# V matmuls of the high and low gate parts side by side, 32 tokens by row in the second expert layer, five places for V's tiles, and x loaded behind four modulation tiles

## The chip, the core and the metric

The kernel runs on one core of a Trainium2 chip. The metric is the time of one execution on the device in microseconds, lower is better. The inputs and weights lie in HBM as float32; the result must agree with the float32 reference.

## The reference, cut to what matters

A two-layer block (mixing layers that the change hardly touches, each followed by an expert layer) runs before a second block. All the change's edits but one are in the expert layer `peer`, which runs twice for 256 tokens of 1024 values:

```python
q = jnp.einsum('td,dhk->thk', x_t, w_q).reshape(T, PEER_HEADS, 2, PEER_HALF)
s = jnp.einsum('thpk,hpnk->thpn', q, sub_keys).astype(jnp.float32)
sv, si = lax.top_k(s, K)                       # 16 of 128, for each half
...
fv, fpos = lax.top_k(cand, K)                  # 16 experts of 16384 per token and head
eidx = jnp.take_along_axis(cidx, fpos, axis=-1)
gate = jax.nn.softmax(fv, axis=-1)
u = u_emb[eidx]
v = v_emb[eidx]
act = jax.nn.gelu(jnp.einsum('thkd,td->thk', u, x_t).astype(jnp.float32), approximate=False)
return jnp.einsum('thk,thkd->td', (gate * act).astype(x_t.dtype), v)
```

Around it stands `x = x + g2 * peer(rmsnorm(x) * (1 + sc2) + sh2)`, where `sc2`, `sh2`, `g2` and their like come from `silu(c) @ ada_w`, the modulation.

## The kernel before

**Dense and by row.** Each token uses 8 x 16 = 128 of the 16384 experts. The kernel does not gather for most tokens: for ND = 240 of the 256 tokens it multiplies with all experts. In the U stage 128 tiles of U (128 experts each) give the activations of every expert for the 240 tokens (`lin_t("ut")`, matmuls at L370), and a sparse gate, spread out by small matmuls of one-hot vectors (`spread`, L1010, four tokens a group, 60 groups), zeroes all but the chosen ones. In the V stage the gated activations, tile by tile, are multiplied with the 128 tiles of V. The first SP = 16 tokens of each layer go by row: GpSimd gathers rows of U and V by index (`fetch`, L1076, 128 rows of 4 KB a gather, 16 gathers of U and 16 of V), VectorE multiplies and adds them (L1140, L1147), and a small matmul with `folds` (L1152) adds the result to the V sums.

**Float32 by parts.** Every dense product is made of three matmuls in the reduced format fp32r: high times high, low times high, high times low. ScalarE makes the high part of a weight tile (`whi`, L90), VectorE the low part (`wlo`, L97). In the V stage ScalarE and VectorE split the gated activations in the same way (`split_w`: `gh` L1020, `gl` L1021, 128x240 each). For a tile of V and each of 8 output blocks c of 128 columns, `into` and `mm3` issue L307 (`whi`, `gh`), L308 (`whi`, `gl`) and L309 (`wlo`, `gh`), each with 240 columns moving and a weight load of 128 columns of its own. Two blocks c share one PSUM bank; the V stage holds the four banks of pool `psa`, for all 128 tiles, and `turn_over` adds the sums to x at its end (L577).

**The order.** A `Stream` loads weight tiles on SyncE's queue in a fixed order (L65), as far as its pools have places: `raw` has three, modulation tiles (`ada`) go to `spare` places in the V stages. Three `whi` and three `wlo` buffers lie behind it, so `wlo` of tile i+2 can be written when TensorE has left tile i-1. Engines work in program order. In tile i of the V stage VectorE does first what `bg.pump` gives it of the work by row (one operation for each 1300 ns of credit; 450 ns of credit per tile in layer 0, 600 in layer 1), then `gl` of tile i+2, then `wlo` of tile i+2, with modulation steps (L217) between. The gathers have two places in layer 0 and three in layer 1; a gather is issued when VectorE has done the operation that used its place.

**The start.** SyncE issues `cols`, `ident`, `x` (1 MB) and then 16 modulation tiles of 512 KB. VectorE makes `folds`, then waits for the norm of x (square on ScalarE L2011, sum on TensorE L456, root L462, reciprocal L463, spread L469), multiplies x with it (L2014) and only then takes the 16 modulation steps (L217). The first weight product (L307 with `hh`) needs all 16.

## Time and profile before

| what | value |
|---|---|
| time, median of 3 runs (lowest to highest) | 2401.97 us (2401.54 to 2405.57) |
| profiled execution: its own time, its span | 2400.41 us, 2398.7 us |
| busy share of the span: PE, PEld, DVE, ACT, POOL | 97%, 95%, 78%, 57%, 5% |
| start, until the first weight product | 0 to 37 us |
| first layer's U stage with its routing, V stage | about 110 to 572 us, 572 to 918 us |
| second layer's U stage with its routing, V stage | about 1100 to 1558 us, 1558 to 1912 us |

A matmul's record in the trace is longer than the step from one matmul to the next, because matmuls overlap: L307 to L309 show 276 ns each, while one starts every 112 ns or so. So what a matmul costs is read from the distance of starts in a stretch without waits, not from the mean duration. For VectorE, too, the distance of starts is what an operation costs in a row of others.

### The profile page before, as it was taken

To read this page: it belongs to the slowest core of one execution; us is meant where nothing else is said; L and a number is where in the kernel's file an instruction comes from. 1 tells how busy PE (TensorE), PEld (TensorE's weight loads), DVE (VectorE), ACT (ScalarE), POOL (GpSimd) and SP (SyncE) were. 2 spreads that over 40 slices of the span, in tenths; PEclk is the share of its full clock that TensorE was granted. 3 is DMA by queue.
4 is the path that set the end of the run, shared out by engine and by line. 5 is a ranking of instruction groups with operands and counts; after the bars stand their busy time and mean duration, and the time that the engine had idled before them with its cause. 6 is when DMAs were issued, how large, how long until landed. Compare 5 with 4: busy or idle time off the path is not lost. (4 is left out here: it accounts for less than half of the span.)

```text
span 2398.7 us, 49306 instructions
## 1 busy us (share of the span) xinstructions
PE 2334.3 (97%) x19476; PEld 2282.8 (95%) x19476; DVE 1877.6 (78%) x3608; ACT 1364.8 (57%) x2598; POOL 130.6 (5%) x151
## 2 busy tenths in 40 slices
PE   4999999999999999999999999999999998999998
PEld 4899999999999999889999999999999987999998
DVE  7979888998888878777889789887766677366854
ACT  4565557875554557666565678754455563345543
POOL 0000100000112100000010000012300001000000
PEclk8999999999999999999999999999999999899999
DMA  9666664447999976446566544588876553054664
GB/s 382 241 190 185 203 187 146 141 141 249 326 332 324 324 267 205 149 150 198 179 196 188 173 140 140 175 283 292 296 220 195 185 163 106 4 168 140 182 194 135
DMA packets 134776, 485.26 MB, mean 202 GB/s; under 512 B 16280, under 2 KB 17560, under 8 KB 133648
## 3 DMA queue, kind: packets, MB, share of 16 engines
q1 hardware_dynamic: 122320, 439.53, 56.9%
q0 software_dynamic: 12224, 42.57, 5.2%
q8 instruction: 153, 2.51, 0.4%
q14 instruction: 79, 0.65, 0.1%
HBM read 477.69 MB, written 3.41 MB: 201 GB/s over the span
## 5 line engine op out<-in xcount | busy, mean ns | idle before, releaser
L97 DVE TENSOR_TENSOR wlo<-raw,whi 128x1024 fp32r<-128x1024 f32 x701 | 854.1, 1219 | 259.5 <-ACT whi L90 257.2
L90 ACT ACTIVATE whi<-raw 128x1024 fp32r<-128x1024 f32 x701 | 737.0, 1052 | 251.9 <-DMA raw<-in_v_dram 130.1
L370 PE MATMUL pa<-hh,whi 128*128 128x240 f32 (+2 forms) x2904 | 816.1, 283 | 0.1
L370 PE MATMUL pa<-hl,whi 128*128 128x240 f32 (+2 forms) x2904 | 795.3, 277 | 0.0
L370 PE MATMUL pa<-hh,wlo 128*128 128x240 f32 (+2 forms) x2904 | 793.5, 278 | 0.3 <-DVE wlo L97 0.3
L309 PE MATMUL pa<-gh,wlo 128*128 128x240 f32 x2000 | 551.7, 276 | 4.4 <-DVE wlo L97 3.9
L307 PE MATMUL pa<-gh,whi 128*128 128x240 f32 x2000 | 552.1, 276 | 0.3 <-ACT whi L90 0.3
L370 PEld LDWEIGHTS pa<-hh,whi 128*128 128x128 f32 x2904 | 549.5, 189 | 2.8 <-issue 1.7
L370 PEld LDWEIGHTS pa<-hl,whi 128*128 128x128 f32 x2904 | 549.8, 190 | 1.0 <-DVE hl L581 0.8
L308 PE MATMUL pa<-gl,whi 128*128 128x240 f32 x2000 | 549.7, 275 | 0.0
L370 PEld LDWEIGHTS pa<-hh,wlo 128*128 128x128 f32 x2904 | 544.4, 189 | 0.9 <-DVE wlo L97 0.9
L309 PEld LDWEIGHTS pa<-gh,wlo 128*128 128x128 f32 x2000 | 378.3, 189 | 6.9 <-DVE wlo L97 6.7
L307 PEld LDWEIGHTS pa<-gh,whi 128*128 128x128 f32 x2000 | 379.2, 190 | 0.6 <-ACT whi L90 0.5
L308 PEld LDWEIGHTS pa<-gl,whi 128*128 128x128 f32 x2000 | 378.6, 189 | 0.0
L1003 ACT ACTIVATE hot<-hot,wij 128x128 f32<-128x128 f32 x480 | 153.7, 396 | 40.8 <-DVE hot L995 40.1
L982 ACT ACTIVATE wl<-pa 128x240 f32<-128x240 f32 x144 | 53.3, 370 | 153.0 <-PE pa L370 152.7
L1010 PE MATMUL pb<-hot 128*128 128x128 f32 x960 | 123.2, 275 | 0.0
L1010 PEld LDWEIGHTS pb<-hot 128*128 128x128 f32 x960 | 115.4, 192 | 0.0
L993 DVE TENSOR_TENSOR hot<-iota,wij 128x512 f32<-128x512 f32 x120 | 82.0, 683 | 35.6 <-PE pb L1010 35.6
L1020 ACT ACTIVATE gh<-wu 128x240 fp32r<-128x240 f32 x112 | 45.1, 403 | 112.2 <-PE pa L309 111.1
L1020 ACT ACTIVATE gh<-wl 128x240 fp32r<-128x240 f32 x142 | 56.5, 398 | 70.0 <-PE pa L309 66.1
L995 DVE TENSOR_TENSOR hot<-iota,wij 128x512 f32<-128x512 f32 x120 | 81.9, 682 | 0.0
(579 smaller groups left out, 3205.1 us busy)
## 6 DMA issues: line engine op xcount, KB each, us to landing
raw<-in_ut_dram SPq DMA_DIRECT2D x256, 512.0 KB, 3.7
raw<-in_v_dram SPq DMA_DIRECT2D x256, 512.0 KB, 4.8
sp<-in_ada_dram SPq DMA_DIRECT2D x56, 512.0 KB, 6.5
ada<-in_ada_dram SPq DMA_DIRECT2D x40, 512.0 KB, 10.2
raw<-in_peer_q_dram SPq DMA_DIRECT2D x32, 512.0 KB, 4.3
raw<-in_up_dram SPq DMA_DIRECT2D x32, 512.0 KB, 4.2
raw<-in_down_dram SPq DMA_DIRECT2D x32, 512.0 KB, 4.2
raw<-in_od_in_dram SPq DMA_DIRECT2D x24, 512.0 KB, 4.2
```

What stands on the lines that cost most here:

```text
L90: self.nc.scalar.activation(hi[:, :width], t[:, :width], AF.Copy)
L97: self.nc.vector.tensor_tensor(lo, t, hi, op=OP.subtract)
L307: PE.matmul(ps, lhsT=lh, rhs=rh, start=start, stop=False)
L308: PE.matmul(ps, lhsT=lh, rhs=rl, start=False, stop=False)
L309: PE.matmul(ps, lhsT=ll, rhs=rh, start=False, stop=stop)
L370: PE.matmul(ps, lhsT=part[a], rhs=part[b], start=start and i == 0, stop=stop and i == len(names) - 1)
L982: ACT.activation(t[:, k, gtok:], ps[:, gtok:], AF.Gelu)
L993: V.tensor_tensor(pm, iota[:, None, :].to_broadcast([128, 4, 128]), wij[:, 2, t0:t0 + 4, None].to_broadcast([128, 4, 128]), op=OP.is_equal)
L995: V.tensor_tensor(qm, iota[:, None, :].to_broadcast([128, 4, 128]), wij[:, 1, t0:t0 + 4, None].to_broadcast([128, 4, 128]), op=OP.is_equal)
L1003: ACT.activation(qm[:, j], qm[:, j], AF.Copy, scale=wij[:, 0, t:t + 1])
L1010: PE.matmul(ps[:, j * 128:j * 128 + 128], lhsT=pm[:, j], rhs=qm[:, j], start=True, stop=True)
L1020: ACT.activation(gh, t[:, k], AF.Copy)
```

## The change

1. **Wide V matmuls.** `gh` and `gl` become the two halves of one tile `g` of 2 x ND columns. For a tile i below 108 + c, block c takes one matmul of `whi` with all of `g` and one of `wlo` with its first half. That needs a bank for each c, so the V stage takes the four banks of `psb` besides. At tile 107 + c the two halves of the sum are added to x by VectorE (two operations on ND columns), and from tile 108 + c on the block works with three matmuls as before, starting its sum again in the first half.
2. **SP = 32 in layer 1** (16 stays in layer 0): ND is 224 there, 56 groups of one-hots instead of 60, and 64 gathers and operations by row instead of 32. The gates of 32 tokens lie on 4 x 32 partitions instead of 8 x 16.
3. **Places for V's tiles.** A pool `more`: in layer 1 two tiles from tile 10 on (five places with `raw`), in layer 0 the tile `htok` from tile 72 on, once the gathers of U are used up (four places).
4. **Credits and points.** 400 ns per tile in layer 0 and 760 in layer 1; the work by row is flushed at tile 118 instead of 120; the gain row is made at tile 104 instead of 100; `folds` is made at the start of each V stage instead of at the kernel's.
5. **The start.** Four modulation tiles are issued ahead of x, and eight modulation steps stand ahead of the norm.

```diff
-SP = 16
-ND = S - SP
+SPS = (16, 32)
...
-    vv = w("v", 0)
+    vv = [e[:4] + ("more" if i >= 72 and i % 4 > 2 else "raw",) for i, e in enumerate(w("v", 0))]
...
-    vv = w("v", 1)
+    vv = [e[:4] + ("more" if i >= 10 and i % 5 > 2 else "raw",) for i, e in enumerate(w("v", 1))]
...
-            def split_w(i, gh=None, gl=None):
+            def split_w(i, g=None):
                 t, k = tile_at(i)
...
+                    g = two.tile([128, 2 * ND], FR, name="g", bufs=3)
+                ACT.activation(g[:, :ND], t[:, k], AF.Copy)
+                V.tensor_tensor(g[:, ND:], t[:, k], g[:, :ND], op=OP.subtract)
...
-            order = [(t, k) for t in ("u", "v") for k in range(16)]
+            order = [(t, k) for t in ("u", "v") for k in range(SP)]
...
-            pss = [acc() for _ in range(4)]
...
+            pss = [acc() for _ in range(4)] + [bank() for _ in range(4)]
...
+                pools["more"] = (Slots([two.tile([128, 1024], FT, name=f"more{k}") for k in range(2)]), 2)
...
-                    into(pss, c, w, *parts_of[i], i == 0, i == 127, SP)
+                    g, cs, n = parts_of[i], slice(c * 128, c * 128 + 128), WIDE + c
+                    if i < n:
+                        PE.matmul(pss[c][:, SP:SP + 2 * ND], lhsT=w[0][:, cs], rhs=g, start=i == 0, stop=False)
+                        PE.matmul(pss[c][:, SP:S], lhsT=w[1][:, cs], rhs=g[:, :ND], start=False, stop=i == n - 1)
+                        if i == n - 1:
+                            for a in (S, SP):
+                                o, ps = x[:, c, SP:], pss[c][:, a:a + ND]
+                                V.scalar_tensor_tensor(o, ps, grow[:, c:c + 1], o, op0=OP.mult, op1=OP.add)
+                    else:
+                        mm3(pss[c][:, SP:S], w[0][:, cs], w[1][:, cs], g[:, :ND], g[:, ND:], i == n, i == 127)
...
-                if i == 120:
+                if i == 118:
                     bg.flush()
...
-                    bg.pump(450 if l == 0 else 600)
+                    bg.pump(400 if l == 0 else 760)
...
+    st.load(4)
     nc.sync.dma_start(x, A["x"])
-    V.tensor_reduce(folds, ident.rearrange("p (h t) -> p t h", t=SP), axis=AX.X, op=OP.add)
     st.load()
...
+    for _ in range(8):
+        st.advance()
     rms(rtok, sums(xs))
```

Below, TensorE in the middle of layer 1's V stage, two blocks c of one tile, before (the letters behind `pa_` are the bank's tile, `gh` and `gl` the activations' parts):

```order
L307 MATMUL pa_20221<-gh_21435,whi_21439 128x240
L308 MATMUL pa_20221<-gl_21436,whi_21439 128x240
L309 MATMUL pa_20221<-gh_21435,wlo_21440 128x240
L307 MATMUL pa_20222<-gh_21435,whi_21439 128x240
L308 MATMUL pa_20222<-gl_21436,whi_21439 128x240
```

and after:

```order
L1170 MATMUL pa_19162<-g_19437,whi_19440 128x448
L1171 MATMUL pa_19162<-g_19437,wlo_19441 128x224
L1170 MATMUL pb_19163<-g_19437,whi_19440 128x448
L1171 MATMUL pb_19163<-g_19437,wlo_19441 128x224
L1170 MATMUL pb_19164<-g_19437,whi_19440 128x448
```

Three matmuls per block became two, with two weight loads instead of three, and each block has a bank of its own.

VectorE in layer 1's V stage, before, at the end of the work by row (`sp` with `act` is one such operation, L1147; `gl` and `wlo` prepare tile i+2):

```order
L1021 TENSOR_TENSOR gl_22246<-wl_14000,gh_22245 128x240
L97 TENSOR_TENSOR wlo_22250<-raw_22147,whi_22249 128x1024
L1021 TENSOR_TENSOR gl_22280<-wl_14000,gh_22279 128x240
L97 TENSOR_TENSOR wlo_22284<-raw_22183,whi_22283 128x1024
L1147 SCALAR_TENSOR_TENSOR sp_20228<-sp_20228,act_20343 128x1024
L1021 TENSOR_TENSOR gl_22317<-wl_14000,gh_22316 128x240
L97 TENSOR_TENSOR wlo_22321<-raw_22217,whi_22320 128x1024
```

and after, at tiles 107 to 109, where the first blocks are added to x (L1175):

```order
L1024 TENSOR_TENSOR g_21953<-wu_16337,g_21953 128x224
L96 TENSOR_TENSOR wlo_21957<-more1_19168,whi_21956 128x1024
L1175 SCALAR_TENSOR_TENSOR x_107<-pa_19159,mod_96,x_107 128x224 x2
L1024 TENSOR_TENSOR g_21979<-wu_16337,g_21979 128x224
L96 TENSOR_TENSOR wlo_21983<-raw_21857,whi_21982 128x1024
L1175 SCALAR_TENSOR_TENSOR x_107<-pa_19160,mod_96,x_107 128x224 x2
L1156 SCALAR_TENSOR_TENSOR sp_19146<-sp_19146,act_19246 128x1024
L1024 TENSOR_TENSOR g_22008<-wu_16337,g_22008 128x224
L96 TENSOR_TENSOR wlo_22012<-raw_21883,whi_22011 128x1024
L1175 SCALAR_TENSOR_TENSOR x_107<-pa_19161,mod_96,x_107 128x224 x2
```

The additions to x stand behind `wlo` of tile i+2, and the work by row, which now reaches to these tiles, stands between.

VectorE at the start, before:

```order
L2002 TENSOR_REDUCE folds_92<-ident_86 128x16
L463 RECIPROCAL rtok_100<-rtok_100 128x2
L2014 TENSOR_TENSOR xs_170<-x_108,nrm_99 128x2048
L217 ISA ada_119,mod_97<-ada_119,cact0_154 128x1024
L217 ISA mod_97 128x1
```

and after, from the last of the first eight steps on:

```order
L215 ISA ada_131,mod_96<-ada_131,cact0_152 128x1024
L215 ISA mod_96 128x1
L464 RECIPROCAL rtok_99<-rtok_99 128x2
L2034 TENSOR_TENSOR xs_168<-x_107,nrm_98 128x2048
L215 ISA ada_133,mod_96<-ada_133,cact0_152 128x1024
```

Half of the 16 modulation steps moved ahead of the reciprocal and of the multiplication of x.

## Rows read from the trace of the kernel before

**Rows 1.** The page: busy time, share of the span and instructions of the engines.
```profile
PE 2334.3 (97%) x19476; PEld 2282.8 (95%) x19476; DVE 1877.6 (78%) x3608; ACT 1364.8 (57%) x2598; POOL 130.6 (5%) x151
```
**Rows 2.** Windows (stretch, length, busy PE, PEld, DVE, ACT, POOL; clock, DMA share, GB/s).
```profile
575.00:920.00 345.00, 342.60 (x3032) 340.97 (x3031) 284.76 (x402) 175.23 (x255) 39.11 (x30) 1.00 0.89 310
1360.00:1565.00 205.00, 205.00 (x1819) 205.00 (x1818) 180.31 (x349) 158.49 (x454) 3.32 (x3) 1.00 0.50 153
1565.00:1915.00 350.00, 347.71 (x3077) 346.21 (x3076) 250.84 (x334) 180.31 (x265) 39.42 (x32) 1.00 0.75 246
```
**Rows 3.** Timeline of TensorE (start, duration): 240 columns, V stage, 91 starts.
```profile
599.80 0.27 PE L309 MATMUL pa<-gh,wlo 128*128 128x240 f32 x1
...
609.91 0.28 PE L309 MATMUL pa<-gh,wlo 128*128 128x240 f32 x1
```
**Rows 4.** The same, 512 columns, 58 starts.
```profile
41.73 0.39 PE L307 MATMUL pa<-whi,hh 128*128 128x512 f32 x1
...
54.95 0.39 PE L307 MATMUL pa<-whi,hh 128*128 128x512 f32 x1
```
**Rows 5.** The same, 256 columns, 87 starts.
```profile
2299.80 0.28 PE L307 MATMUL pa<-ah,whi 128*128 128x256 f32 x1
...
2309.98 0.28 PE L309 MATMUL pa<-ah,wlo 128*128 128x256 f32 x1
```
**Rows 6.** The same, 64 columns in float32, nine rows of two; weight loads ahead of 16.
```profile
2097.77 0.39 PE L1869 MATMUL pb<-sa,lt 128*128 128x64 f32 x2
...
2099.78 0.39 PE L1868 MATMUL pb<-vC,mk 128*128 128x64 f32 x2
...
832.03 1.86 PEld L1152 LDWEIGHTS pa<-folds,sp 128*128 128x128 f32 x16
833.81 0.19 PEld L307 LDWEIGHTS pa<-gh,whi 128*128 128x128 f32 x1
```
**Rows 7.** The same, two groups of one-hot matmuls in the U stage.
```profile
1440.09 1.95 PE L1010 MATMUL pb<-hot 128*128 128x128 f32 x16
1441.80 0.36 PE L370 MATMUL pa<-hh,whi 128*128 128x240 f32 x1
```
**Rows 8.** Timeline of the start, all engines (in brackets: idle before, and what ended it).
```profile
7.28 2.55 ACT L2011 ACTIVATE xs<-x 128x256 f32<-128x256 f32 x8
...
13.83 0.17 DVE L463 RECIPROCAL rtok<-rtok 128x2 f32<-128x2 f32 x1 [10.28 <-ACT rtok L462]
...
15.21 2.29 DVE L2014 TENSOR_TENSOR xs<-x,nrm 128x2048 f32<-128x2048 f32 x1 [1.22 <-ACT nrm L471]
17.42 1.22 DVE L217 CUSTOM_DVE_ANT_0 ada<-ada,cact 128x1024 f32<-128x1024 f32 x1
...
28.88 1.06 ACT L90 ACTIVATE whi<-ada 128x1024 fp32r<-128x1024 f32 x1 [13.70 <-DMA ada<-in_ev_in_dram]
...
35.76 0.08 DVE L217 DVE_READ_ACCUMULATOR2_ANT mod<- 128x1 f32 x1
```
**Rows 9.** Windows up to the first layer's U stage (columns as in rows 2).
```profile
10.00:15.00 5.00, 2.87 (x23) 2.48 (x22) 0.17 (x1) 1.75 (x3) 0.00 (x0) 1.00 1.03 415
...
60.00:70.00 10.00, 9.63 (x66) 8.62 (x65) 10.00 (x14) 5.27 (x7) 0.00 (x0) 1.00 1.02 407
```
**Rows 10.** Timeline of VectorE: one operation by row, U's; additions to x.
```profile
1601.56 1.22 DVE L1140 CUSTOM_DVE_ANT_0 rows<-rows,htok 128x1024 f32<-128x1024 f32 x1
...
1602.70 0.40 DVE L1021 TENSOR_TENSOR gl<-wl,gh 128x240 fp32r<-128x240 f32 x1
...
106.02 0.88 DVE L577 SCALAR_TENSOR_TENSOR x<-pa,mod,x 128x256 f32<-128x256 f32 x2
```
**Rows 11.** Timeline of ScalarE and VectorE late in layer 1's V stage.
```profile
1887.91 0.40 ACT L1020 ACTIVATE gh<-wu 128x240 fp32r<-128x240 f32 x1 [1.35 <-PE pa L309]
...
1889.29 1.22 DVE L97 TENSOR_TENSOR wlo<-raw,whi 128x1024 fp32r<-128x1024 f32 x1 [0.54 <-ACT whi L90]
```
**Rows 12.** Time from issue to landing of the gathers, both layers.
```profile
DMA to landing us min/median/max: 5.0/6.8/9.8
```

More of the change, by code (lines that the diff above doesn't have):

```diff
@@ L200, in col @@
         return cols[:, a + i:a + i + n]
-    folds = cst.tile([128, SP], FT, name="folds")
     consts = cst.tile([128, 2], FT, name="consts")
@@ L300, in net @@
     entries += w("up") + w("down")
-    pools = {"raw": (rawp, 3), "ada": (None, 0), "spare": (None, 0)}
+    pools = {"raw": (rawp, 3), "ada": (None, 0), "spare": (None, 0), "more": (None, 0)}
     st = Stream(nc, pools, hip, lop, entries)
@@ L411, in __init__, with block @@
             self.nxt, self.extra = nxt, extra
+        def block(self, c):
+            return block(self.pss, c)
         def mm(self, k, w, c):
@@ L576, in turn_over @@
                 for j in (k, k + 1):
-                    V.scalar_tensor_tensor(x[:, j], block(lk.pss, j), grow[:, j:j + 1], x[:, j], op0=OP.mult, op1=OP.add)
+                    V.scalar_tensor_tensor(x[:, j], lk.block(j), grow[:, j:j + 1], x[:, j], op0=OP.mult, op1=OP.add)
             for j in (k, k + 1):
@@ L937, in peer_route @@
             V.scalar_tensor_tensor(pk[:SP, :, 1], sel[:SP, 0], 128.0, sel[:SP, 1], op0=OP.mult, op1=OP.add)
+            n = SP // 16
             for h in range(8):
-                G.dma_start(picks[h * SP:h * SP + SP], pk[:SP, h])
+                G.dma_start(picks[h // n * SP:h // n * SP + SP, :, h % n * 16:h % n * 16 + 16], pk[:SP, h])
             yield 300
@@ L949, in peer @@
     def peer(l, x, hT, nxt):
+        SP = SPS[l]
+        ND = S - SP
         with ExitStack() as es:
@@ L952, in peer @@
             wl = low.tile([128, I0, ND], FT, name="wl")
-            picks = low.tile([128, 2, 16], FT, name="picks")
-            pick = low.tile([128, 16], I32, name="pick")
+            picks = low.tile([128, 2, SP], FT, name="picks")
+            pick = low.tile([128, SP], I32, name="pick")
             htok = low.tile([128, 1024], FT, name="htok")
@@ L969, in by_token @@
                     ACT.activation(htok[:SP, q * 512:q * 512 + 512], ps[:SP], AF.Copy)
-                for h in range(1, 8):
+                for h in range(1, 128 // SP):
                     G.dma_start(htok[h * SP:h * SP + SP], htok[:SP])
@@ L1053, in route @@
                             yield from peer_top(s_sb, h, b, rs[b], pool)
-                        yield from peer_route(rs[b], wij, pool, b, picks)
+                        yield from peer_route(rs[b], wij, pool, b, picks, SP)
                         if b == 0:
@@ L1096, in peer @@
                     first = again(low, "wij", 3, 256)
-                    split_w(0, first[:, 0, :ND], first[:, 1, :ND])
+                    split_w(0, first.rearrange("p a t -> p (a t)")[:, :2 * ND])
                 old = spread_
@@ L1128, in peer @@
                 rows.places.append(places[2])
+                pools["more"] = (Slots([two.tile([128, 1024], FT, name=f"more{k}") for k in range(2)]), 2)
             def sparse():
-                act = two.tile([128, 16], FT, name="act")
+                act = two.tile([128, SP], FT, name="act")
                 while len(got) < len(rows.places):
@@ L1145, in sparse, with block @@
                         V.tensor_scalar(ysp, r, act[:, 0:1], None, op0=OP.mult)
+                        if l == 0:
+                            pools["more"] = (Slots([htok]), 1)
                     else:
                         V.scalar_tensor_tensor(ysp, r, act[:, k:k + 1], ysp, op0=OP.mult, op1=OP.add)
-                    if n + ahead < 32:
+                    if n + ahead < len(order):
                         got.append(fetch(*order[n + ahead]))
                     yield 1300
-                for c in range(8):
-                    PE.matmul(block(pss, c)[:, :SP], lhsT=ysp[:, c * 128:c * 128 + 128], rhs=folds, start=False, stop=False)
-                yield 0
+            folds = two.tile([128, SP], FT, name="folds")
+            V.tensor_reduce(folds, ident.rearrange("p (g t) -> p t g", t=SP), axis=AX.X, op=OP.add)
             bg.set(sparse())
             class Outs:
-                def __init__(self):
-                    self.pss = pss
                 def mm(self, i, w, c):
-                    into(pss, c, w, *parts_of[i], i == 0, i == 127, SP)
+                    g, cs, n = parts_of[i], slice(c * 128, c * 128 + 128), WIDE + c
[8 more added lines that the diff above has]
+                        mm3(pss[c][:, SP:S], w[0][:, cs], w[1][:, cs], g[:, :ND], g[:, ND:], i == n, i == 127)
+                def block(self, c):
+                    return pss[c][:, :S]
                 def finish(self, c):
@@ L1174, in peer @@
             for i in range(126):
-                if i == 100:
+                if i == 104:
                     grow = ada_done(l, 5)
-                if i == 120:
+                if i == 118:
                     bg.flush()
+                    for c in range(8):
+                        PE.matmul(pss[c][:, :SP], lhsT=ysp[:, c * 128:c * 128 + 128], rhs=folds, start=False, stop=False)
                 if i == 124:
@@ L1192, in peer @@
                 parts_of.pop(i)
-            pools["spare"] = (None, 0)
+            pools["spare"] = pools["more"] = (None, 0)
             sq = wu.rearrange("p i t -> p (i t)")[:, :2048].rearrange("p (k t) -> p k t", k=8)
```

12 lines of the change are left out of this document (4 added, 8 removed).

## The prediction

> **What bounds the kernel now.** First the page's busy times: TensorE 97%, its weight loads 95%, VectorE 78% [rows 1]. Then windows by stage, since an average hides stages: in both V stages, and in the U stage with one-hots, TensorE is busy at full granted clock nearly all the time, while VectorE has 17 to 28% of the V stages free [rows 2]. So a microsecond off TensorE's queue in these stages is a microsecond off the end, as long as nobody else becomes late. The start is another matter: there TensorE waits for VectorE.
>
> Then the real price of a matmul, from distances of starts: 240 columns, 10.11 us over 90 steps, 112.3 ns [rows 3]; 256 columns, 10.18 over 86, 118.4 ns [rows 5]; 512 columns, 13.22 over 57, 231.9 ns [rows 4]. From 256 to 512 that is 0.443 ns a column. But the line doesn't go on below 240: records with 64 columns take 2.01 us over 18 steps, 111.7 ns, and sixteen weight loads for matmuls of only 16 columns take 1.78 us, 111 ns each [rows 6]. What is common to them is a weight load of 128 columns. I read this as a floor: a matmul with its own full weight load costs some 111.5 ns, however few columns move. At 240 columns kernel and floor are level. This decides what each half of the change is worth.
>
> **The change part by part.**
> *Wide matmuls, layer 0.* Sum over c of (108 + c) is 892 blocks with two matmuls, 132 keep three. Before, 3 x 112.3 = 336.9 ns. After, 480 columns by the line between 256 and 512: 118.4 + 224 x 0.443 = 217.6, and 240 columns 112.3; together 329.9. Saved: 7.0 ns x 892 = 6.2 us. Bounds of the unseen 480: twice the 240, 224.6, saves nothing; 256's price plus its columns at the slope between 240 and 256 (6.1 ns / 16 = 0.38), 203.5, saves 18.8 us. I take the line, since both its ends are measured.
>
> *Wide matmuls, layer 1.* 448 columns: 118.4 + 192 x 0.443 = 203.5; 224 columns: the floor, 111.5. Together 315.0, saved 21.9 x 892 = 19.5 us; the 132 triples save 3 x 0.8 each, 0.3 us. Here 32 tokens by row pay: the wide matmul is 32 columns shorter and not on the floor. Bounds: 209.6 for 448 (twice 112.3 less 32 x 0.468, the 240's price per column) with 112.3 leaves 13.4 us; 191.4 by the slope 0.38 leaves 30.3.
>
> *U stage, layer 1.* 128 x 8 x 3 = 3072 matmuls go from 240 to 224 columns. By the floor they save 0.8 ns each, 2.5 us; nothing if the floor is 112.3; 18.7 us if the slope 0.38 went on. I take 2.5, because 64 and 16 columns cost the same [rows 6]. Four groups of one-hots fewer: two groups take 1.71 us [rows 7], so 3.4 us off TensorE, which was busy all 205 us there [rows 2].
>
> The Trainium skill ("TensorE: Matmul & The Clock Gate", LDWEIGHTS) gives a load as its columns divided by 1.2, 106.7 ns for 128. The rows lie at 111 to 112; by the page's figure the 3072 would cost 5.6 ns less each, 17 us in place of 2.5, and the sum below would be lower by that. The measured floor decides, and nothing below uses the page.
>
> *Start.* x now lands behind 2.1 MB of modulation, which at 415 GB/s [rows 9] is 5.1 us. The squares start at 12.4 instead of 7.28 [rows 8]; the reciprocal came 6.55 us after that, now at 18.9. The eight steps ahead of it need four more tiles behind x, again 5.1 us, so the last ends near 17.5 + 1.15 = 18.6: level, they hide in the 10.28 us that VectorE was idle. Then 1.38 to the multiplication, 2.21 for it, and eight steps of (35.76 - 17.42) / 16 = 1.146: 18.9 + 1.4 + 2.2 + 9.2 = 31.7, against 35.76. 4.1 us earlier. The first weight tile is there at 28.88 [rows 8], so it isn't late next. Afterwards VectorE is busy without gaps [rows 9], so what it gains stays; DMA is full at 407 GB/s too, which is the lower bound (nothing gained, if tiles come no earlier). Upper bound: half the steps off, 9 us.
>
> *Additions to x, new.* At tile 107 + c VectorE adds two halves to x, and block c's next matmul, one tile later, waits for them. Two such operations cost 0.88 us in a row at 256 columns [rows 10]. They stand behind `wlo` of tile i+2, which starts 1.38 us after its tile's turn of the buffers and takes 1.14 [rows 11]: done some 2.5 us into the tile, 3.4 with the additions. TensorE is back at block 0 after 8 x 0.33 = 2.64 us in layer 0 and 2.52 in layer 1: it waits about 0.9 us once; for later c its way is 0.3 us longer each and the wait fades. In layer 1 the work by row still runs here (1.14 us an operation [rows 10], one in 1.7 tiles), behind which `g` and `wlo` of the next tile queue. I put 1.5 us for layer 0, 2.5 for layer 1; bounds 0 and 8 x 0.88 = 7 each.
>
> *Work by row, layer 1.* 32 more operations of 1.14 us are 36.5, the additions 7 more. VectorE goes from 251 to about 294 us, over a stage that shrinks to 330: 89%, layer 0 was at 83% without loss [rows 2]. A late gather holds VectorE, and `g` and `wlo` behind it, then TensorE. I put 2.5 us. The bytes grow by 32 gathers of 0.52 MB to some 310 GB/s, what layer 0 carried on three places; five places cover a landing that gets longer. `folds` costs two small reductions, hidden or 0.4 us; the other edits nothing, since the flush at 118 finds the work by row already done (64 x 1300 / 760 = 110 tiles).
>
> *Sum.* 6.2 + 19.5 + 0.3 + 2.5 + 3.4 + 4.1 = 36.0 off; 1.5 + 2.5 + 2.5 + 0.4 = 6.9 on; 29.1 net. From the profiled execution's 2400.4 that is 2371.3; the median of the runs was 1.6 higher, so **2373 us**.
>
> **Rivals.**
> *No floor, columns alone set the price.* For: 240 to 256 still costs 0.38 ns a column. Against: rows 6. The U stage would give 18.7 instead of 2.5, the 224s in V 892 x 5.3 = 4.7 more, the triples 2: 23 lower, 2350. [...]
>
> *Wide matmuls cost what their columns cost at 240.* For: between 256 and 512 the price per column is hardly lower (0.453 against 0.463). Then the doing away with a weight load gives nothing in layer 0 (6.2 lost) and 13.4 - 19.5 in layer 1: 2385. This is the case in which the first edit doesn't do what it seems made for.
>
> *The gathers become the bound, slower.* Layer 1 has three places for 64 gathers. One operation in 1.7 tiles of 2.52 us is one in 4.3 us, so a place must turn round in 12.9: issue and landing, now 6.8 in the median and 9.8 at most [rows 12], the operation, and the queue on VectorE. With 3 us for the last two, it decides from a landing of about 10 us. If the fuller DMA made it 13, a turn would be 16, 5.3 us an operation, and the stage 64 x 1.0 = 64 us longer: 2437. Against: the longest landing seen, under the heavier load of layer 0 included, stays just below the point, and landing in the median has 3 us to spare.
>
> *The start gains nothing* because the DMA queue is the bound: 2377, inside the range.
>
> **How the numbers follow.** Forecast, with small errors of each term: 0.69. Columns alone: 0.10. Wide matmuls at 240's rate: 0.13. Gathers: 0.08, half of it mild (a few us to 35 lost), half beyond. The forecast's own range is 2362 to 2383. To hold 0.8 with a part of both neighbours I take 2354 to 2388. A measurement tells 0.2%, 4.8 us, from no change: faster than 2397 in all of the first three and some mild gather cases, 0.93; same 0.03; slower than 2407 0.04.
>
> **What would show it.** In the V stages, starts 217 ns after a 480-column matmul and 203 after 448, and 111 to 112 after a 224-column one; in layer 1's U stage still 111 to 113 a step. Steps of 105 to 107 there mean columns alone; 224 after 480 means the second rival. At the start, the last of 16 modulation steps near 31.7. At tiles 108 to 112, waits of TensorE's wide-to-narrow change for the additions to x, about 1 us at most. In layer 1's V stage, VectorE waiting for gathers, and TensorE for `wlo` by more than 5 us in all, would show the third rival. If V's gain in layer 1 is there and the total is not, I have mis-seen a wait behind the stages.

## The result, and the profile after

The changed kernel takes **2367.76 us** in the median of four runs (2366.22 to 2369.46), the kernel before 2401.76 beside it (four runs, 2393.81 to 2405.57): a ratio of 0.9868, 95% interval 0.9852 to 0.9883, 34 us less. In the larger groups of runs below, the kernel before has medians of 2398.26 to 2400.23, which would make it 30.5 to 32.5 us less. The forecast was 2373, with a range of 2354 to 2388. The profiled execution shown here took 2369.46 us, its span is 2367.8, 30.9 below the span of before.

The page first: busy time, share of the span and instructions of each engine, against [rows 1].

```profile
PE 2304.9 (97%) x17660; PEld 2210.4 (93%) x17660; DVE 1914.7 (81%) x3673; ACT 1351.0 (57%) x2578; POOL 211.3 (9%) x179
```

TensorE has 1816 matmuls fewer and is busy as large a share as before; VectorE has 37 us more to do in a shorter span. So the kernel is bound as it was. The windows of layer 0's V stage and of layer 1's U stage and V stage (columns as in [rows 2]):

```profile
575.00:905.00 330.00, 324.67 (x2012) 293.94 (x2012) 278.49 (x398) 164.56 (x241) 41.95 (x30) 1.00 0.88 314
1360.00:1550.00 190.00, 190.00 (x1703) 189.98 (x1702) 167.71 (x322) 144.11 (x420) 3.25 (x3) 1.00 0.47 155
1550.00:1880.00 330.00, 327.88 (x2192) 312.67 (x2192) 285.29 (x394) 175.25 (x263) 118.37 (x62) 1.00 0.87 315
```

The third line is the one to look at. VectorE went from 72% to 86% of that stage, the DMA from 246 to 315 GB/s, and TensorE still waits for only 2 us of 330. In the first line TensorE waits for 5.

Where the time went, by landmarks, each the first or last start of a line of matmuls in the two traces:

| stretch | before | after | difference |
|---|---|---|---|
| start to first score matmul (first scores of layer 0) | 126.3 | 125.4 | -0.9 |
| from there to the first one-hot matmul of layer 0 | 242.7 | 243.8 | +1.1 |
| from there to the first attention matmul behind layer 0 (the end of its U stage, its V stage, and 83 us more) | 637.4 | 636.8 | -0.6 |
| last score matmul to last one-hot matmul of layer 1 (U stage) | 387.6 | 379.3 | -8.3 |
| from there to an attention of the second block (V stage of layer 1, and some 255 us more) | 625.9 | 602.6 | -23.3 |
| first to last V matmul of layer 0 alone | 351.5 | 352.0 | +0.5 |
| first to last V matmul of layer 1 alone | 350.8 | 330.8 | -20.0 |

Layer 1 has it all in this pair of traces. Of its last stretch, 20.0 us lie in the V stage itself and 3.0 behind it, where nothing was edited. The prices behind it, from distances of starts as in [rows 3 to 5]. Timeline of TensorE in layer 0, the first rows of 61 and the last one:

```profile
599.77 0.38 PE L1170 MATMUL pb<-g,whi 128*128 128x480 f32 x1
599.99 0.28 PE L1171 MATMUL pb<-g,wlo 128*128 128x240 f32 x1
600.10 0.38 PE L1170 MATMUL pb<-g,whi 128*128 128x480 f32 x1
...
609.75 0.38 PE L1170 MATMUL pa<-g,whi 128*128 128x480 f32 x1
```

Thirty pairs in 9.98 us: 332.7 ns a pair, 220 for the wide matmul and 112 for the other. The forecast was 329.9. The same for layer 1, from the first wide matmul to the eightieth:

```profile
1599.88 0.37 PE L1170 MATMUL pb<-g,whi 128*128 128x448 f32 x1
1600.09 0.27 PE L1171 MATMUL pb<-g,wlo 128*128 128x224 f32 x1
1600.19 0.37 PE L1170 MATMUL pb<-g,whi 128*128 128x448 f32 x1
...
1624.81 0.37 PE L1170 MATMUL pb<-g,whi 128*128 128x448 f32 x1
```

79 pairs in 24.93 us: 315.6 ns, forecast 315.0. The split is another than forecast (212 and 103, against 203.5 and 111.5), the sum is right.

### The profile page after: what moved, and what is told of

Its sections match the earlier page's. It is cut to its first block, busy times and chain, and to the rows that moved or that the text cites. A ratio compares the mean times of both kernels' runs of the same rounds, so it can differ in the third digit from the quotient of the medians.

```text
span 2367.8 us, 46020 instructions
## 1 busy us (share of the span) xinstructions
PE 2304.9 (97%) x17660; PEld 2210.4 (93%) x17660; DVE 1914.7 (81%) x3673; ACT 1351.0 (57%) x2578; POOL 211.3 (9%) x179
## 5 line engine op out<-in xcount | busy, mean ns | idle before, releaser
L368 PE MATMUL pa<-hh,whi 128*128 128x224 f32 (+3 forms) x2904 | 813.5, 282 | 0.2 <-ACT hh L545 0.2
L368 PE MATMUL pa<-hl,whi 128*128 128x224 f32 (+3 forms) x2904 | 794.5, 277 | 0.1
L368 PE MATMUL pa<-hh,wlo 128*128 128x224 f32 (+3 forms) x2904 | 792.1, 278 | 1.5 <-DVE wlo L96 1.5
L1170 PE MATMUL pb<-g,whi 128*128 128x480 f32 (+1 forms) x900 | 304.1, 378 | 0.0
L1170 PE MATMUL pa<-g,whi 128*128 128x480 f32 (+1 forms) x868 | 293.9, 378 | 0.0
L1171 PE MATMUL pb<-g,wlo 128*128 128x240 f32 (+1 forms) x900 | 242.9, 270 | 0.0
L1171 PE MATMUL pa<-g,wlo 128*128 128x240 f32 (+1 forms) x868 | 235.3, 271 | 4.2 <-DVE wlo L96 4.1
L1170 PEld LDWEIGHTS pb<-g,whi 128*128 128x128 f32 x900 | 169.4, 188 | 20.8
L1171 PEld LDWEIGHTS pa<-g,wlo 128*128 128x128 f32 x868 | 165.2, 190 | 7.9 <-DVE wlo L96 7.6
L1171 PEld LDWEIGHTS pb<-g,wlo 128*128 128x128 f32 x900 | 171.1, 190 | 0.0
L1014 PEld LDWEIGHTS pb<-hot 128*128 128x128 f32 x928 | 111.7, 192 | 0.0
```

The lines of the kernel that those rows point to most:

```text
L368: PE.matmul(ps, lhsT=part[a], rhs=part[b], start=start and i == 0, stop=stop and i == len(names) - 1)
L1014: PE.matmul(ps[:, j * 128:j * 128 + 128], lhsT=pm[:, j], rhs=qm[:, j], start=True, stop=True)
L1170: PE.matmul(pss[c][:, SP:SP + 2 * ND], lhsT=w[0][:, cs], rhs=g, start=i == 0, stop=False)
L1171: PE.matmul(pss[c][:, SP:S], lhsT=w[1][:, cs], rhs=g[:, :ND], start=False, stop=i == n - 1)
```

## The experiments

All are the kernel before or the changed kernel with one thing undone, doubled or taken away. The ratios are to the kernel before, timed in the same group of runs.

**1. Which part brings it: 16 tokens by row in layer 1.** The changed kernel with SP = 16 in both layers. The two extra places of layer 1 don't fit into SBUF then, because the tiles of 2 x 240 columns are larger, so layer 1 gets layer 0's form, `htok` as a fourth place from tile 72 on.

```diff
-SPS = (16, 32)
+SPS = (16, 16)
-    vv = [e[:4] + ("more" if i >= 10 and i % 5 > 2 else "raw",) for i, e in enumerate(w("v", 1))]
+    vv = [e[:4] + ("more" if i >= 72 and i % 4 > 2 else "raw",) for i, e in enumerate(w("v", 1))]
-                    bg.pump(400 if l == 0 else 760)
+                    bg.pump(400)
```

> The changed kernel with 16 tokens by row in layer 1 too (credit 400 there; without the shorter gate tiles there is no room for two more places, so V has a fourth place from tile 72 on, as in layer 0). Theory (a matmul costs its columns or, below some 240, its weight load of about 112 ns; wide matmuls save the third load): layer 1 goes the way of layer 0, a block costs 332.7 ns in place of 315.3, so its V stage is about 16 us longer than in the changed kernel (346 for 330), its U stage 9 us longer (113.6 ns a step for 111.7, four groups more): about 2393 us, that is 8 us under before or less. Rival (the gain of layer 1 comes from the wide matmuls and the places as such, not from the tokens): V stage of layer 1 still 335 us or less, about 2375 us.

Measured: 2391.07 us, before 2398.26; ratio 0.9975 (0.9963 to 0.9988). The U stage of layer 1 took 387.6 us, as before, and the V stage with what follows 616.5, 9.4 less than before (the V stage alone 344.5). So about a fifth of the gain, 7 of 34 us, comes with 16 tokens by row; the rest needs the 32. It is not the two places that this kernel lacks: these are all of TensorE's waits in layer 1's V stage, and they are for the additions to x.

```profile
PE pa L305 <- DVE x L1171: 1.3, 2, 1.0
```

**2. No wide matmuls.** The changed kernel with three matmuls a block throughout, all else kept.

```diff
-                    if i < n:
-                        PE.matmul(pss[c][:, SP:SP + 2 * ND], lhsT=w[0][:, cs], rhs=g, start=i == 0, stop=False)
-                        PE.matmul(pss[c][:, SP:S], lhsT=w[1][:, cs], rhs=g[:, :ND], start=False, stop=i == n - 1)
...
-                    else:
-                        mm3(pss[c][:, SP:S], w[0][:, cs], w[1][:, cs], g[:, :ND], g[:, ND:], i == n, i == 127)
+                    mm3(pss[c][:, SP:S], w[0][:, cs], w[1][:, cs], g[:, :ND], g[:, ND:], i == 0, i == 127)
```

> The changed kernel without wide matmuls: three matmuls of 224 or 240 columns per block throughout, nothing added to x ahead of the end; 32 tokens, places, start kept. Theory: a block of layer 1 costs 3 x 111.7 = 335 ns in place of 315.3, 17.6 us more over 892 blocks, less 3 us of waits for the additions; layer 0 is unchanged, since what its wide matmuls save (3.8 us) is spent in waits: about +15 us, 2383. Rival (columns alone set the price): a block of 3 x 224 columns would cost what 448 + 224 cost, and the time stays within 4 us of the changed kernel's 2368.

Measured: 2383.57 us, ratio 0.9939 (0.9919 to 0.9959). In layer 1 the V stage takes 344.8 us against 330.8 with wide matmuls: they are worth 14.0 us there (15.7 with what follows). In this kernel 2958 matmul records fill layer 1's V window without a gap:

```profile
1550.00:1880.00 330.00, 330.00 (x2958) 330.00 (x2956) 273.84 (x360) 165.90 (x247) 77.10 (x62) 1.00 0.87 308
```

**3. Three places for V's tiles.** The changed kernel without `more` in both layers.

```diff
-    vv = [e[:4] + ("more" if i >= 72 and i % 4 > 2 else "raw",) for i, e in enumerate(w("v", 0))]
+    vv = w("v", 0)
-    vv = [e[:4] + ("more" if i >= 10 and i % 5 > 2 else "raw",) for i, e in enumerate(w("v", 1))]
+    vv = w("v", 1)
```

> The changed kernel with V's tiles in three places throughout. Theory (the places are needed, since gathers and tiles together move 315 GB/s in layer 1 and a place must turn round in 3 x 2.52 = 7.6 us): TensorE waits for wlo in layer 1's V stage by 5 to 25 us, ScalarE waits for V's tiles in more than half the tiles; 2373 to 2393 us. Rival (places are cover that nothing needs): within 2 us of 2368, waits of TensorE for wlo under 3 us.

Measured: 2400.28 us, ratio 1.001 (0.9994 to 1.0025). More than expected: without the places **nothing is left of the gain**. The window of layer 1's V stage, and the longest waits of ScalarE and of the weight loads in it (time, number, longest):

```profile
1550.00:1880.00 330.00, 312.76 (x1968) 289.29 (x1966) 267.60 (x370) 163.68 (x243) 105.21 (x63) 0.99 0.84 301
```

```profile
ACT whi L89 <- DMA raw<-in_v_dram: 114.3, 76, 4.2
...
PEld pa L1171 <- DVE wlo L96: 19.0, 24, 1.3
```

In the changed kernel the first of these is 5.5 us, in 5 waits. The chain is landing, `whi`, `wlo`, TensorE: TensorE is the last in it, and it waits 17 us in this window. The V stage of layer 1 takes 355.8 us, 25 more than in the changed kernel. That of layer 0, which has three places throughout here as well, takes 354.0; the mean of five with the fourth place is 348.7.

**4. Is it three, four or five?** The changed kernel with one extra place in layer 1 in place of two.

```diff
-    vv = [e[:4] + ("more" if i >= 10 and i % 5 > 2 else "raw",) for i, e in enumerate(w("v", 1))]
+    vv = [e[:4] + ("more" if i >= 10 and i % 4 > 2 else "raw",) for i, e in enumerate(w("v", 1))]
-    pools["more"] = (Slots([two.tile([128, 1024], FT, name=f"more{k}") for k in range(2)]), 2)
+    pools["more"] = (Slots([two.tile([128, 1024], FT, name=f"more{k}") for k in range(1)]), 1)
```

> The changed kernel with four places for V's tiles in layer 1 (one extra place, every fourth tile from 10 on) in place of five; three gave 2400. Theory: what counts is whether a place can turn round, landing (4.5 us in the median before) plus the wait for ScalarE and the two splits (some 3 us), within the number of places times a tile's 2.52 us: 7.6 for three, too little, 10.1 for four, enough in the median. So most of the 32 us comes back: 2368 to 2376. Rival: the longest landings decide, not the median, and each place gives its share, so about half comes back: 2380 to 2388.

Measured: 2366.05 us (2363.41 to 2370.55), before 2400.23; ratio 0.9864 (0.9838 to 0.989), the same as with five. ScalarE waits 9.7 us for V's tiles in that stage, in 9 waits, and TensorE is busy for 326.98 of 330:

```profile
1545.00:1875.00 330.00, 326.98 (x2184) 311.50 (x2183) 284.91 (x393) 175.80 (x262) 114.29 (x62) 1.00 0.86 314
```

The step lies between three and four; the fifth place buys nothing that can be measured. That fits the theory that a place must turn round within the places times a tile's 2.52 us, though the theory's own sum does not decide it: landing, 4.5 us in the median in layer 1's V stage of before, and about 3 for ScalarE's and VectorE's splits (1.05 and 1.22 us) and their queues make 7.5, level with the 3 x 2.52 = 7.6 that three places give. Experiment 3 shows the turn: 355.8 us for 128 tiles are 2.78 us a tile, so three places turned round in 8.3 us in the mean. Four places give 4 x 2.52 = 10.1.

**5. 32 tokens by row in layer 0 too.**

```diff
-SPS = (16, 32)
+SPS = (32, 32)
-                    bg.pump(400 if l == 0 else 760)
+                    bg.pump(760)
```

> The changed kernel with 32 tokens by row in layer 0 too (credit 760, two places for its 64 gathers, three for V's tiles up to tile 72, 40 modulation steps besides). Rival (TensorE alone bounds both V stages): layer 0's U stage 9 us and its V stage 15 us shorter, 2344 us. Theory (VectorE and the gathers' turn bound that stage: 278 + 38 us of VectorE in a stage of some 330, a gather's place must turn round in 2 x 4.3 = 8.6 us against a landing of 7 plus the operation): the U stage gives 9 us, the V stage gives nothing or gets longer by up to 25 us, with TensorE waiting for wlo by more than 15 us: 2360 to 2385 us.

Measured: 2391.21 us, ratio 0.9971 (0.9958 to 0.9984). Layer 0's V stage, with its two gather places and 48 modulation steps in it, takes 383.3 us, 31.3 more than in the changed kernel; 5.5 of them come back at the end of the U stage, with its four groups of one-hots fewer. In the window TensorE is busy for 296 of 330, and VectorE waits for gathers:

```profile
575.00:905.00 330.00, 295.96 (x1758) 267.93 (x1757) 285.96 (x410) 149.50 (x219) 121.09 (x61) 0.97 0.92 342
```

```profile
DVE sp L1156 <- DMA rows<-in_v_dram,pick: 19.4, 15, 3.8
PE pa L1171 <- DVE wlo L96: 18.4, 26, 1.7
```

This is the forecast's third rival, the gathers as the bound, in the layer that has two places for them. Is it near in layer 1 too?

**6. Two gather places in layer 1.** The changed kernel with one place taken away.

```diff
-                rows.places.append(places[2])
```

> The changed kernel with two places for gathered rows in layer 1's V stage in place of three. An operation of the work by row comes every 4.3 us, so a place must turn round in 8.6 us; landing took 6.8 us in the median and 9.8 at most before, the operation 1.1. Theory of the third rival (a gather that is late holds VectorE, and wlo behind it, then TensorE, nearly one for one): about 8 to 9.5 us a turn, 64 operations, 0 to 30 us slower, about 15: 2383. Other theory: VectorE's 12% of free time and the three g tiles ahead take it up, 2368 to 2371.

Measured: 2402.88 us, before 2399.49; ratio 1.0022 (1.0009 to 1.0035), all of the gain gone again, a little beyond the upper end expected. From layer 1's last one-hot matmul to the second block's attention it takes 638.8 us, 36.2 more than the changed kernel, 32.9 of them in the V stage itself. VectorE's waits in that stage:

```profile
DVE sp L1155 <- DMA rows<-in_v_dram,pick: 29.9, 19, 3.9
DVE rows L1145 <- DMA rows<-in_u_dram,pick: 24.8, 13, 4.0
```

In the changed kernel VectorE has no wait for a gather there. The 64 operations run from 1551.1 to 1857.2 us, 63 steps of 4.86 us: two places turn round in **9.7 us**. With three places, in the changed kernel, they run from 1557.4 to 1830.5, 4.33 us a step, which is the pace that the credits set; a turn could last 13.0. So the rival's mechanism is real, and three places stand 3 us away from it.

**7. The floor, further down.** The changed kernel with 64 tokens by row in layer 1: 192 columns in the U stage, 384 and 192 in V.

```diff
-SPS = (16, 32)
+SPS = (16, 64)
-                    bg.pump(400 if l == 0 else 760)
+                    bg.pump(400 if l == 0 else 1500)
```

> The changed kernel with 64 tokens by row in layer 1 (credit 1500), so that the U stage's matmuls have 192 columns and V's 384 and 192. Theory (a matmul with its own weight load of 128 columns has a floor near 111.6 ns): a step of the U stage stays at 111 to 112 ns at 192 columns. In the V stage 128 operations of 1.14 us bring VectorE from 285 to about 358 us of work, above TensorE's some 290, and three gather places have to turn round 128 times: that stage takes 30 to 75 us longer, the one-hots some 7 us less: 2390 to 2440. Rival (columns alone set the price): a step of the U stage falls to about 98 ns, 3072 of them save 40 us, and the time is 2350 to 2400.

Measured: 2461.14 us, ratio 1.0258 (1.0232 to 1.0284), 21 us beyond the upper end expected. The U stage settles the floor. Timelines of TensorE in the U stage, 137 starts each, first the changed kernel and then this one:

```profile
1171.81 0.27 PE L368 MATMUL pa<-hh,whi 128*128 128x224 f32 x1
...
1186.99 0.27 PE L368 MATMUL pa<-hl,whi 128*128 128x224 f32 x1
```

```profile
1171.75 0.28 PE L368 MATMUL pa<-hl,whi 128*128 128x192 f32 x1
...
1186.94 0.27 PE L368 MATMUL pa<-hh,wlo 128*128 128x192 f32 x1
```

15.18 and 15.19 us over 136 steps, 111.6 and 111.7 ns: 32 columns fewer bring nothing. By columns alone it would have been 98. The Trainium skill ("TensorE: Matmul & The Clock Gate", LDWEIGHTS) puts the load of 128 columns at 106.7 ns; the step measured here is 5 ns longer.

In the V stage of this kernel the same 192 columns stand behind a wide matmul, and there they go below that floor: from the second row to the third it is 90 ns (89 in the median), from the first to the second 200 (198).

```profile
1565.86 0.36 PE L1170 MATMUL pa<-g,whi 128*128 128x384 f32 x1
1566.06 0.25 PE L1171 MATMUL pa<-g,wlo 128*128 128x192 f32 x1
1566.15 0.36 PE L1170 MATMUL pa<-g,whi 128*128 128x384 f32 x1
```

In the V stage as a whole the gathers pace VectorE: the operations run from 1545.0 to 1926.5 us, 127 steps of 3.00 us, a turn of 9.0 us for three places, and TensorE is last in line. It stands idle for 74 of the 420 us, and its granted clock (first of the last three columns) is 0.90 in the mean; how much that adds to the time is not known.

```profile
1540.00:1960.00 420.00, 346.29 (x2117) 327.95 (x2115) 348.49 (x477) 166.00 (x253) 224.68 (x126) 0.90 0.88 323
```

**8. The start alone.** The kernel before with the new order of the start.

```diff
     nc.sync.dma_start(ident, A["ident"])
+    st.load(4)
     nc.sync.dma_start(x, A["x"])
...
         ACT.activation(xs[:, k], x[:, k], AF.Square)
+    for _ in range(8):
+        st.advance()
```

> The kernel before with one part of the change alone: x behind four modulation tiles, and eight modulation steps ahead of the row sums. Theory: the DMA queue is full from 10 to 90 us in both kernels, so VectorE's earlier steps are given back while it waits for tiles. The first weight product then starts near 34.5 us (37.1 before), the first score matmul (line 840) near 125.4 (126.2 before), the first hot matmul (line 1010) at 369.0 within 0.5, and the time is that of before within 1 us (about 2400). Rival (my forecast): the 2.5 us or more stay: first score matmul near 123.5, hot near 366.5, time about 2397.

One execution: 2393.46 us. First weight product at 33.8 us (37.1 before), first score matmul 124.5 (126.3), first one-hot matmul 367.1 (369.0). So 3.2 us at the first product, and nearly half of it lost by the time of the scores; that lies between the theory and the rival. The total was lower than that explains, because the stretch with layer 0's V stage, where nothing was edited, took 633.2 us and not 637.4. So the same kernel was run more often:

> The kernel of the first look at the start alone once more, timed in rounds. That look showed the first weight product 3.2 us earlier, the first score matmul 1.8 us and the first hot matmul 1.9 us earlier, and a further 4 us in layer 0's V stage, where the edit changes nothing. Theory: the edit is worth 1 to 2 us, the rest is scatter between executions: ratio 0.9985 to 1.0. Rival: the 4 us belong to it too: ratio near 0.997.

Measured: 2397.87 us (12 runs), before 2400.23 (16 runs); ratio 0.999 (0.9977 to 1.0003). Its first score matmul starts at 125.4 in that profile. By the landmarks the edit is worth 1 to 2 us. The time alone says less: its interval reaches from 5.5 us gained to 0.7 lost, so it excludes neither nothing nor the 4.1 of the forecast. The rival's ratio of 0.997 lies just outside it, so the 4 us of layer 0 are scatter as far as this shows.

**9. Why half of it is lost.** Two kernels, with the old and with the new start, that load only half of each of the first 40 modulation tiles.

```diff
+            if j < 40:
+                for _ in range(2):
+                    V.tensor_tensor_reduce(t[:, :512], t[:, :512], cact[0][:, :512], scale=1.0, scalar=0.0,
+                                           op0=OP.mult, op1=OP.add, accum_out=mod[:, j:j + 1])
+                return
...
+            return [(("ada", l * 48 + j), A["ada"][l * 48 + j][:, :512], 512, ada_step(l * 48 + j), src) for j in js]
```

> The kernel before, but of the first 40 modulation tiles only the first 512 of 1024 columns are loaded, and each step is taken twice over that half, so that VectorE's columns stay the same while the bytes of this stretch fall by 40 x 0.26 = 10.5 MB, 25 us at 408 GB/s (half of the modulation's input is left out of the sum, so the output isn't the reference's). It is the partner of the next kernel; what counts is the difference of the two. Theory (DMA is the bound of the first 90 us): the first score matmul moves from 126.2 to about 115 or less, until VectorE's steps (1.15 us, 40 of them) are the bound. If DMA isn't the bound, it stays at 124 to 127.

> The same halved modulation tiles, with the changed start (x behind four tiles, eight steps ahead of the row sums); half of the modulation's input is left out of the sum here too. Theory (bytes gave the gain back): with fewer bytes the queue runs ahead, and the changed start keeps 2 to 4 us at the first score matmul against the kernel with the old start. Rival (something behind the start, not the bytes, sets the time): the two agree within 1 us at the first score matmul, as they do with whole tiles.

Measured: 2409.13 us with the old start, 2399.12 with the new one, one execution each. My first expectation missed: the score matmul did not come earlier with half the bytes but later, at 136.0, because two half steps take VectorE 1.35 us from start to start where a whole one takes 1.15, 8 us over 40 tiles, and VectorE became the bound. With half tiles the new start keeps all that it gains: first weight product 41.7 and 34.6 (-7.2), first score matmul 136.0 and 128.9 (-7.1), first one-hot matmul 379.2 and 371.4 (-7.8). The DMA share (last column but one) falls as well. From 10 to 90 us, the changed kernel and the one with half tiles and the new start:

```profile
10.00:90.00 80.00, 56.69 (x299) 49.10 (x300) 71.05 (x123) 37.63 (x63) 0.91 (x1) 0.81 1.01 404
```

```profile
10.00:90.00 80.00, 54.12 (x281) 46.05 (x282) 72.15 (x177) 36.90 (x62) 1.39 (x1) 0.83 0.83 290
```

But the pair does not show that the bytes take the gain. The queue is full with whole tiles, yet between 38 and 90 us neither TensorE nor VectorE nor ScalarE waits for a DMA, in the kernel before, in the changed one or in the two executions of experiment 8. What differs is the clock of TensorE over its first 16 weight products, 512 columns each. In this order the kernel before, the changed kernel, half tiles with the old start, half tiles with the new one (granted clock: first of the last three columns):

```profile
37.06:42.66 5.60, 5.54 (x16) 4.05 (x17) 5.10 (x10) 5.50 (x11) 0.00 (x0) 0.70 1.03 410
34.48:41.40 6.92, 6.86 (x16) 5.02 (x17) 6.07 (x12) 6.50 (x11) 0.00 (x0) 0.54 1.03 410
41.74:47.66 5.92, 5.86 (x16) 4.30 (x17) 5.41 (x10) 5.83 (x11) 1.36 (x1) 0.65 0.84 257
34.58:40.64 6.06, 6.00 (x16) 4.37 (x17) 5.56 (x10) 5.97 (x11) 1.39 (x1) 0.64 0.87 281
```

In each of them TensorE comes out of 13 us of idle time or more at a granted clock of 0.50 (1.2 GHz) and later rises to 1.00 (2.4 GHz), at 40.4, 40.8, 45.9 and 39.0 us. So it runs its products at the low level for 3.4 us before and 6.3 after, and the same 16 products take 1.3 us longer: half of the 2.6 us gained. With half tiles the two stretches happen to be alike, 4.1 and 4.4 us, and the loss is 0.1. In all ten executions with whole tiles and the new start the 16 products take 6.8 to 7.1 us. With whole tiles and the old start there is only the one trace, so how often its low stretch is as short as 3.4 us is not known.

## Why the prediction was right, and where its terms were off

The direction, the mechanism and the total were right: 2373 for 2367.76, and 29.1 us net for the 34 measured (30.5 to 32.5 beside the larger groups of before). That the total came so near is partly luck, since the terms are off with both signs. The two profiles side by side, and the means of all the profiles whose code is that of before or that of after in the stretch (how many, in brackets):

| stretch | forecast, net | two profiles | means |
|---|---|---|---|
| start, to the first scores | -4.1 | -0.9 | -1.1 (1 and 10) |
| V stage, layer 0 | -4.5 | +0.5 | -1.3 (5 and 5) |
| U stage, layer 1 | -5.9 | -8.3 | -8.3 (6 and 6) |
| V stage, layer 1 | -14.6 | -20.0 | -17.3 (5 and 3) |

(The forecast's 0.4 for `folds`, half in each V stage, is counted in.) The V stages go from the first to the last V matmul. Behind each of them the changed kernel gains another 1.5 to 2 us in the means, up to the next attention. The forecast has no term for that, and no run shows where it comes from.

**Wide matmuls, layer 1: right.** Before, the steps that do not follow a wait have a mean of 112.3 ns over the whole stage, as in [rows 3]; after, a block costs 315.6 ns over all 892. That makes 21.3 x 892 = 19.0 us, forecast 19.5. Two of the signs named did not come, 203 ns after 448 columns and 111 to 112 after 224: it was 212 and 103. Only the sum was right. That is more than chance, since it holds at three shapes: 332.3 ns for 329.9 at 480 and 240 columns, 315.6 for 315.0 at 448 and 224, 287 for 286.6 (the same line and floor) at 384 and 192. Why the wide matmul takes up what the narrow one gives is not shown.

**The rest of layer 1's V stage: the term that failed is the wait for the work by row.** I charged 2.5 us for it and 2.5 for the additions. All of TensorE's waits in that stage after, by reason:

```profile
PE pa L305 <- DVE x L1175: 1.8, 3, 1.2
PE pa L1171 <- DVE wlo L96: 0.3, 1, 0.3
```

The first are the additions, in the place and of the kind that was forecast: the longest first, 1.2 us, then fading. With the slower steps right behind each wait they cost 2.5 us, as charged. The work by row cost at most the 0.9 us that is left of the slow steps, and VectorE has no wait for a gather. In the trace of before the waits of that stage, with the slow steps behind them, come to 4.2 us and in that of after to 3.4. So 19.0 + 0.2 for the triples + 4.2 - 3.4 = 20.0, which is the whole of what the stage lost. But 4.2 belongs to one execution. TensorE's busy time in this stage in the trace of before, and in one of experiment 9 with the same code there:

```profile
1558.30:1909.20 350.90, 348.63 (x3091) 347.40 (x3090) 249.28 (x331) 180.59 (x265) 39.35 (x32) 1.00 0.76 249
1570.60:1917.50 346.90, 346.90 (x3091) 346.82 (x3090) 249.54 (x331) 181.14 (x265) 39.34 (x31) 1.00 0.76 252
```

In four other executions with the code of before the waits cost 0.3 to 2.7 us. So it is not shown that the extra places took waits away that were there before; they are cover, as forecast. Experiment 3 shows how far the cover is from nothing: its absence costs 32 us, and I had named the landing that "gets longer" without a price for it.

**U stage, layer 1: right in kind, too small.** Four groups of one-hots were 3.4, measured 3.3. For the 3072 matmuls I took the floor for what they cost after, and it was right (111.6, forecast 111.5). What they cost before was mis-sized, 113.6 and not 112.3, in 135 starts in the trace of before:

```profile
1171.76 0.28 PE L370 MATMUL pa<-hh,whi 128*128 128x240 f32 x1
...
1186.98 0.28 PE L370 MATMUL pa<-hh,wlo 128*128 128x240 f32 x1
```

I had carried a price from the V stage to the U stage, in which the same 240 columns run 1 ns slower. From the last score to the last one-hot matmul 2944 of the matmuls took 337.5 us before and 332.5 after, 5.0 in place of 2.5, and 5.0 + 3.3 is the 8.3 of the landmarks. The floor itself, the choice against the first rival, is settled by experiment 7; the rival's 2350 is refuted.

**Wide matmuls, layer 0: half of it.** 480 columns took 220 ns and not 217.6, and the pair 332.3, so it saves 336.9 - 332.3 = 4.6 ns, 4.1 us in place of 6.2. From that come off the additions, 2.3 us with the slow steps behind them (forecast 1.5). That leaves 1.8, less `folds`. The two profiles show nothing of it, because TensorE waited longer for `wlo` in that of after:

```profile
PE pa L1171 <- DVE wlo L96: 3.8, 7, 0.8
```

In experiment 6, whose layer 0 has the same code, the same wait is 0.6 us. The stage scatters from one execution to the next: 346.4 to 352.0 us in five with wide matmuls, 346.7 to 352.7 in five with the code of before. The difference of the means, 1.3 us, is no surer than that. Layer 0 is the layer with three places, four in its second half, at 314 GB/s; with three throughout (experiment 3) it took 354.0.

The second rival (wide matmuls at 240's price per column) would have made 480 columns cost 224.6, and 220 lies between it and the forecast; in layer 1, where 448 and 224 cost 315.6 together and not the 321.9 of that rival, it is wrong.

**Start: the step that failed.** The forecast said that VectorE is busy without gaps afterwards, "so what it gains stays", and put a full DMA queue as the lower bound. It followed VectorE alone and had no term for TensorE's clock, and the clock took a part of the gain twice. The rows of before that [rows 8] leave out, row sums and first weight product:

```profile
7.83 4.32 PE L456 MATMUL pb<-consts,xs 128*128 128x128 f32 x32 [1.08 <-ACT xs L2011]
...
37.06 0.80 PE L307 MATMUL pa<-whi,hh 128*128 128x512 f32 x1 [22.30 <-ACT hh L498]
```

The same after, with the reciprocal:

```profile
13.13 5.60 PE L457 MATMUL pb<-consts,xs 128*128 128x128 f32 x32 [6.10 <-ACT xs L2029]
...
20.41 0.17 DVE L464 RECIPROCAL rtok<-rtok 128x2 f32<-128x2 f32 x1 [1.49 <-ACT rtok L463]
...
34.48 0.80 PE L305 MATMUL pa<-whi,hh 128*128 128x512 f32 x1 [13.14 <-ACT hh L499]
```

First, the squares started at 12.57 (forecast 12.4), but the row sums took 5.60 us where they took 4.32 before, and the reciprocal came at 20.4 in place of 18.9. TensorE had been idle for 6.1 us ahead of them, and in the window the granted clock is half, where it was 1.00 in [rows 9]:

```profile
10.00:15.00 5.00, 1.87 (x9) 1.90 (x10) 3.52 (x7) 2.43 (x8) 0.00 (x0) 0.51 1.00 412
```

I had moved x back and not asked what that idle time does to the clock. So the last of the 16 steps ended at 33.2 and not at 31.7 (35.8 before), 2.6 us gained and not 4.1. (In the first execution of experiment 8 the sums took 5.29 us though the windows show a clock of 1.00. They run at 6 to 7 a microsecond up to 16 us and at 10 to 11 behind, as here, and the trace has no record of the clock ahead of a rise at 15.9 us. In the second execution of that kernel the clock is 0.50 from 11 to 17 us and the sums take 5.79.)

Second, TensorE begins its weight products 2.6 us earlier but runs them at the low level for 6.3 us in place of 3.4, which costs 1.3 us (experiment 9). At the next place where TensorE waits for `wlo`, at 57 us, it waits 2.0 us and not 1.7. From there on 0.9 us is left, and it is still 0.9 at the scores. The forecast's lower bound, tiles that come no earlier, is not what happened, since nobody but GpSimd waits for a DMA in that stretch.

**Gathers: right.** The rival's price was a turn of 12.9 us with three places. A turn of 9.0 to 9.7 was measured where gathers are the bound (experiments 6 and 7), so 3 us were to spare, as worked out.

## What to carry to other kernels

A faster consumer needs its tiles sooner: compare the turn of a place (landing, wait and splits) with the number of places times the new time of a tile, leave a margin, and give the places their own price, since here 32 us, nearly the whole gain, hung on the step from three to four. Joining two matmuls that share a weight tile pays where three matmuls stand on the floor of the weight load: 3 x 111.7 = 335.0 ns became 315.6 at 224 columns, while at 240 columns, level with the floor, 336.9 became only 332.3. Before narrowing a matmul, look whether it already stands on that floor. And a gain of one engine is not yet a gain of the kernel: ask which engine runs next, and at what clock it will start.

## What the runs showed of the hardware

- In a chain of its own kind, a matmul with its own weight load of 128 columns has a floor of 111.6 to 111.7 ns in this kernel, at 224 columns and at 192 (experiment 7). Behind a wide matmul, though, the next start comes 103 ns after 224 columns and 89 ns after 192, and the wide one takes the difference (212 ns for 448 columns, 198 for 384). Only the sum of a pair could be worked out from the separate prices.
- The same 240 columns cost 113.6 ns a step in the U stage and 112.3 in the V stage.
- A wait of TensorE costs more than its idle time: the step behind it takes 214 to 219 ns where it takes 112 otherwise (before, both V stages).
- From 10 to 15 us of the changed kernel the granted clock was 0.51, close to 1.2 GHz throughout; TensorE had had no matmul since 7.0 us. The row sums ran at 6 to 7 a microsecond there, against 11 a little later at 1.00. After another 13 us of idle time the first 16 weight products, of 512 columns, took 6.9 us, 6.3 of it at 0.50; in the kernel before, with 3.4 us at 0.50, they took 5.6.
- Where VectorE waits for gathers (33 of 64 operations in experiment 6, 52 of 128 in experiment 7), a place for a gather of 128 rows of 4 KB turns round in 9.0 to 9.7 us in the mean.
